# A delta-rule inverse built from 32-row blocks, w_ada sums issued beside the recurrence, and four scored blocks at the opening of the expert stage

## The chip, the cores and the metric

The kernel runs on one core of a Trainium2 chip. The metric is device time in microseconds (us) from the first to the last instruction, as the median of several runs. PE is TensorE, DVE VectorE, ACT ScalarE, POOL GpSimd, and SP the engine that issues most DMAs.

## What is computed

One decoder layer on 512 tokens of width 1024. Four parts of it matter here:

```python
mod = silu(c) @ w_ada + b_ada                      # six vectors of 1024: shifts, scales, gates
# gated delta rule, by chunks: a unit lower-triangular system for each chunk and head
a_mat = eye + where(strict, kk, 0.0)
sol = triangular_solve(a_mat, [v * beta, kb * exp(gc)])
v_new = u_c - w_c @ state                          # a recurrence over the chunks
o = q_c @ state + attn @ v_new
# PEER: 8 heads pick 16 of 128 x 128 single-neuron experts for each token
act = gelu(h @ expert_u[ids]);  ff = (gates * act) @ expert_v[ids]
x = x + gt2 * ff;  return rms_norm(x, final_norm_w)
```

The kernel uses chunks of 128 tokens (four) for the delta rule, and handles the experts densely for three token tiles (384 tokens): it scores all 128 blocks of 128 experts, multiplies the scores by a gate matrix that is zero where an expert wasn't picked, and adds up the values. The fourth token tile is gathered row by row on POOL and DVE.

## The kernel before

The stages follow one another: normalisation with the first 16 of 48 w_ada sums, projections with the short convolution, the decays and key comparison of each chunk (`decays`, `compare`), the inverse, the recurrence over the chunks, the gMLP and output projection, routing, the building of the gates (with the scores of 47 "early" blocks, written to DRAM as `sgd`), and the expert stage.

**The inverse (L436 to L477).** Each of 16 systems (4 chunks by 4 heads) is a 128x128 matrix `LS`. The inverse `X` and its transpose `Z` grow by doubling, in seven levels: at level `l` the block of `LS` that the mask `lvl[:, l]` lets through (`ms`, DVE, 128x512 for a chunk) is multiplied with `X` (`py`, L456), copied to `Y` by ACT, and multiplied with `Z` and `X` (`pz` L465, `px` L469); DVE adds the changed halves (L471, L473). All are 128x128 by 128x128 products in fp32, which the trace lists as two records each. The seven masks are made in the normalisation stage (L271 to L276). Between the chunks of each level stands a step of `later_sums`: a load of 512 KB of w_ada by SP into one of two buffers and a DVE product with a sum (L204), 32 in all.

**The recurrence (L536 to L600).** Per chunk there are products of 128x128 in fp32 with DVE and ACT steps between. `advance(fill, 13)` issues, after each chunk, 13 steps of projections that don't depend on it (`silu_z`, `gelu_v`, `token_v`); a step of a projection is three matmuls of 512 columns.

**The expert stage (L938 on).** For block `b`: `load_u`, `split_u` (ACT makes the high part, DVE the low part), `expert_scores` (24 matmuls of 384 columns into `pS`, then gelu to `sgl`; a "new" block is scored here, an early one is read back as `sgr`), `gated` (DVE product with the gates, ACT `ahi`, DVE `alo`), `split_v` (`vhi`, `vlo`), and `expert_values` (18 products of 512 columns into `acc`). `kinds` sets which blocks are early. `load_a` loads the gates for eight blocks at a time (1536 KB, DRAM `gd`). `score_ahead` scores two blocks ahead of the values. `finish` adds the residual, normalises and stores a token tile.

**What sets the order.** On PE the order is written by hand from the delta rule to the end; in the expert stage all engines are. In the delta-rule stage a scheduler orders DVE, ACT, POOL and SP.

Of the kernel before, what the change touches and what calls it, by code (L numbers as in the profile page):

```python
# [10 lines left out]
F32 = mybir.dt.float32  # L11
# [13 lines left out]
KD = D // P  # L25
EPS = 1e-6
H = 4
# [10 lines left out]
LAST = 3  # L38
SPARE = 5
# [17 lines left out]
def layer(ctx: ExitStack, tc: tile.TileContext, I, out):  # L57
# [88 lines left out]
    with ExitStack() as mixer:  # L146
# [13 lines left out]
        lvl = act.tile([P, 7, P], F32, name="lvl")  # L160
        ints = uT[:, 3].rearrange("p (a b) -> p a b", a=4).bitcast(I32)
        pi, fi, sj, si = (ints[:, i] for i in range(4))
        nc.gpsimd.iota(pi, pattern=[[0, P]], base=0, channel_multiplier=1)
        nc.gpsimd.iota(fi, pattern=[[1, P]], base=0, channel_multiplier=0)
# [44 lines left out]
        with ExitStack() as n1, tc.manual_schedule(engines={nc.vector.engine}):  # L209
# [61 lines left out]
            for l in range(7):  # L271
                nc.vector.tensor_scalar(sj, pi, l, None, op0=OP.logical_shift_right)
                nc.vector.tensor_scalar(si, fi, l, 1, op0=OP.logical_shift_right, op1=OP.bitwise_xor)
                same = zT[:, 0, :P]
                nc.vector.tensor_tensor(same, si, sj, op=OP.is_equal)
                nc.vector.scalar_tensor_tensor(lvl[:, l], same, -1.0, m2[:, 0], op0=OP.mult, op1=OP.mult)  # L276


        with ExitStack() as gdn, tc.manual_schedule(engines={nc.tensor.engine}):
# [88 lines left out]
            att, X, Z, Y, LS = ([gc_.tile(HP, F32, name=f"{nm}{n}") for n in range(NT)] for nm in ("at", "X", "Z", "Y", "ls"))  # L368
# [70 lines left out]
            idh = bc(ident[:, None, :], HP)  # L439

            def halves(x, l):
                return x.rearrange("p a (b two m) -> p a b two m", two=2, m=2 ** l)


            wad = gdn.enter_context(pool("wad2", 2))
            msum = t4("msum")[:, 0, :32]
            later_sums = mod_sums(range(16, 48), wad, msum, 16)
            for l in range(7):
                for n in range(NT):
                    if l:  # L450
                        advance(later_sums, 1 if n else 2)
                    ms = g2.tile(HP, F32, tag="ms", name="ms", bufs=4)
                    nc.vector.tensor_tensor(ms, LS[n], bc(lvl[:, l:l + 1, :], HP), op=OP.mult)
                    py = bank("py")
                    for h in range(H):
                        mm(py[:, h * P:(h + 1) * P], ms[:, h], X[n][:, h] if l else ident, start=True, stop=True)  # L456
                    if l == 0:
                        nc.vector.tensor_tensor(X[n], heads(py), idh, op=OP.add)
                        nc.vector.tensor_tensor(Z[n], ms, idh, op=OP.add)
                    else:  # L460
                        nc.scalar.copy(flat(Y[n]), py)
                for n in range(NT) if l else ():
                    pz = bank("pz")
                    for h in range(H):
                        mm(pz[:, h * P:(h + 1) * P], Y[n][:, h], Z[n][:, h], start=True, stop=True)  # L465
                    if l < 6:
                        px = bank("px")
                        for h in range(H):
                            mm(px[:, h * P:(h + 1) * P], Z[n][:, h], Y[n][:, h], start=True, stop=True)  # L469
                        xe = halves(X[n], l)[:, :, :, 0]  # L470
                        nc.vector.tensor_tensor(xe, xe, halves(heads(px), l)[:, :, :, 0], op=OP.add)  # L471
                    zo = halves(Z[n], l)[:, :, :, 1]
                    nc.vector.tensor_tensor(zo, zo, halves(heads(pz), l)[:, :, :, 1], op=OP.add)  # L473
# [715 lines left out]
```

## Time and profile before

| | us |
|---|---|
| median of 3 runs (1647.06 to 1648.66) | 1648.52 |
| the profiled execution | 1648.68 |
| its span, first to last instruction | 1647.0 |
| PE busy | 1564.7 |
| DVE busy | 1308.4 |
| ACT busy | 642.7 |

The span is the time that the profiler saw; what lies around it was 1.7 us in that execution. In the trace, an idle time is shown behind the instruction that ended it, with the instruction or transfer that was waited for. The granted clock is the TensorE clock that the throttle let through (1.00 is 2.4 GHz, 0.50 is 1.2 GHz).

### The profile page before, as it was taken

The page shows a single profiled execution, that of the slowest core. Times are in us where ns is not written, and L with a number is a line of the kernel's source. Part 1 is how long each engine was busy: PE and PEld are TensorE (multiplying, and loading weights), DVE is VectorE, ACT ScalarE, POOL GpSimd, SP SyncE. Part 2 cuts the span into 40 slices and gives each one's busy share as a digit, 9 for nine tenths or more (in the row PEclk, how much of TensorE's full clock was granted, in tenths as well). Part 3 has the DMA queues.
Part 4 walks back from the last instruction along what each step waited for, and adds up shares of the span by engine and source line. Part 5 has one row for each costly group of instructions (what it writes and reads, how often), then busy time and mean ns, then how long its engine had stood idle before and what let it go on. Part 6 is the DMA issues. An engine that isn't in the chain of part 4 may idle for free.

```text
span 1647.0 us, 22971 instructions
## 1 busy us (share of the span) xinstructions
PE 1564.7 (95%) x8567; PEld 1382.6 (84%) x8567; DVE 1308.4 (79%) x2463; ACT 642.7 (39%) x928; POOL 478.8 (29%) x355
## 2 busy tenths in 40 slices
PE   5898989999998989997999999999999999999996
PEld 3687978877897978896888888888888888888884
DVE  7989954646999999974688887888887888887756
ACT  4641224344345545562333333333333333333333
POOL 0000000005436600001244444445444444544201
PEclk9998999999998999998999999999999999999998
DMA  9223632334214567767899999999999999998753
GB/s 359 66 66 129 205 125 77 102 132 168 85 43 130 159 222 290 278 264 265 288 336 328 349 354 321 325 340 364 319 342 333 361 333 329 345 355 319 252 186 125
DMA packets 133394, 402.31 MB, mean 244 GB/s; under 512 B 12449, under 2 KB 49185, under 8 KB 131618
## 3 DMA queue, kind: packets, MB, share of 16 engines
q1 hardware_dynamic: 95106, 261.89, 44.3%
q0 software_dynamic: 38176, 138.95, 23.8%
q8 instruction: 67, 1.10, 0.3%
q14 instruction: 45, 0.37, 0.1%
HBM read 362.19 MB, written 38.60 MB: 243 GB/s over the span
## 4 chain that ended last, share of the span: by engine, by line
PE 81%; DVE 10%; DMA 5%; ACT 2%; issue 1%; POOL 1%; SPq 0%; DVEq 0%; ACTq 0%; POOLq 0%
PE pS L75 10%; PE acc L76 10%; PE acc L77 10%; PE pS L77 10%; PE acc L75 10%; PE pS L76 10%; DMA wada<-in_w_ada_c 3%; PE pp L76 3%; PE pp L75 3%; PE pp L77 3%; DVE wada L204 2%; PE pq L76 2%; PE pq L77 2%; PE pq L75 2%; PE pgb L915 1%
## 5 line engine op out<-in xcount | busy, mean ns | idle before, releaser
L972 POOL DMA_INDIRECT u_rows<-in_u_rows,rows x128 | 204.8, 1600 | 562.1 <-DVE dots L979 341.9
L75 PE MATMUL pS<-hhi,uhi 128*128 128x384 f32 x1024 | 356.6, 348 | 1.3 <-ACT uhi L731 1.3
L77 PE MATMUL pS<-hhi,ulo 128*128 128x384 f32 x1024 | 349.6, 341 | 6.1 <-POOL ulo L80 6.1
L76 PE MATMUL pS<-hlo,uhi 128*128 128x384 f32 x1024 | 348.3, 340 | 0.0
L75 PE MATMUL acc<-vhi,ahi 128*128 128x512 f32 x768 | 301.1, 392 | 14.1 <-ACT vhi L1035 14.0
L76 PE MATMUL acc<-vlo,ahi 128*128 128x512 f32 x768 | 302.5, 394 | 1.7 <-DVE vlo L80 1.7
L77 PE MATMUL acc<-vhi,alo 128*128 128x512 f32 x768 | 302.4, 394 | 0.0
L77 PEld LDWEIGHTS pS<-hhi,ulo 128*128 128x128 f32 x1024 | 193.8, 189 | 7.4 <-POOL ulo L80 7.4
L75 PEld LDWEIGHTS pS<-hhi,uhi 128*128 128x128 f32 x1024 | 194.0, 189 | 5.0 <-ACT uhi L731 2.0
L76 PEld LDWEIGHTS pS<-hlo,uhi 128*128 128x128 f32 x1024 | 194.2, 190 | 3.7
L80 DVE TENSOR_TENSOR vlo<-vraw,vhi 128x1024 fp32r<-128x1024 f32 x128 | 156.8, 1226 | 50.0 <-ACT vhi L1035 50.0
L1022 ACT CAST ahi<-a 128x384 fp32r<-128x384 f32 x128 | 65.7, 513 | 332.9 <-DVE a L1020 332.9
L75 PEld LDWEIGHTS acc<-vhi,ahi 128*128 128x128 f32 x768 | 145.4, 189 | 43.8 <-ACT vhi L1035 15.2
L76 PEld LDWEIGHTS acc<-vlo,ahi 128*128 128x128 f32 x768 | 145.1, 189 | 31.8 <-DVE vlo L80 3.0
L77 PEld LDWEIGHTS acc<-vhi,alo 128*128 128x128 f32 x768 | 145.2, 189 | 30.4
L972 POOL DMA_INDIRECT v_rows<-in_v_rows,rows x128 | 149.1, 1165 | 73.9 <-issue 35.6
L989 DVE SCALAR_TENSOR_TENSOR facc<-v_rows,dots,facc 128x1024 f32<-128x1024 f32 x128 | 164.7, 1287 | 0.6
L979 DVE CUSTOM_DVE_ANT_0 junk<-u_rows,h2tok 128x1024 bf16<-128x1024 f32 x128 | 156.0, 1219 | 0.1
L731 ACT CAST uhi<-uraw 128x1024 fp32r<-128x1024 f32 x128 | 133.6, 1047 | 39.0 <-PE pS L76 34.1
L80 POOL TENSOR_TENSOR wlo<-raw,whi 128x1024 fp32r<-128x1024 f32 x14 | 33.7, 2408 | 393.7 <-PE ptx L661 358.8
L751 ACT ACTIVATE sgl<-pS 128x384 f32<-128x384 f32 x128 | 62.6, 489 | 218.4 <-PE pS L77 214.9
L1035 ACT CAST vhi<-vraw 128x1024 fp32r<-128x1024 f32 x128 | 133.9, 1047 | 0.0
(321 smaller groups left out, 2549.8 us busy)
## 6 DMA issues: line engine op xcount, KB each, us to landing
uraw<-in_u_t SPq DMA_DIRECT2D x128, 512.0 KB, 6.4
vraw<-in_v_rows SPq DMA_DIRECT2D x125, 512.0 KB, 5.7
wada<-in_w_ada_c SPq DMA_DIRECT2D x48, 512.0 KB, 4.3
gd<-scs SPq DMA_DIRECT2D x12, 2048.0 KB, 6.6
gates<-gd SPq DMA_DIRECT2D x16, 1536.0 KB, 12.1
raw<-in_w_in_t SPq DMA_DIRECT2D x24, 512.0 KB, 3.3
sgd<-sgl SPq DMA_DIRECT2D x47, 192.0 KB, 3.9
sgr<-sgd SPq DMA_DIRECT2D x47, 192.0 KB, 5.8
```

The source lines that it names most:

```text
L75: mm(o, ahi, bhi, start=start, stop=False)
L76: mm(o, ahi, blo, start=False, stop=False)
L77: mm(o, alo, bhi, start=False, stop=stop)
L80: eng.tensor_tensor(lo, full, hi.bitcast(F32), op=OP.subtract)
L204: nc.vector.tensor_tensor_reduce(w, w, scB, scale=1.0, scalar=0.0 if bias is None else bias[:, c:c + 1], op0=OP.mult, op1=OP.add, accum_ou ...
L731: nc.scalar.copy(hi, raw)
L751: nc.scalar.activation(sgl, pS[:, :TD], AF.Gelu_apprx_tanh)
L972: nc.gpsimd.indirect_dma_start(out=r, out_offset=None, in_=I[src], in_offset=bass.IndirectOffsetOnAxis(ap=rows_[:, j:j + 1], axis=0))
L979: nc.vector.tensor_tensor_reduce(junk, rowsin.pop(("u_rows", j)), h2tok, scale=1.0, scalar=0.0, op0=OP.mult, op1=OP.add, accum_out=dots[j ...
L989: nc.vector.scalar_tensor_tensor(facc, rowsin.pop(("v_rows", j)), d[:, j % GP:j % GP + 1], facc, op0=OP.mult, op1=OP.add)
L1022: nc.scalar.copy(ahi, a)
L1035: nc.scalar.copy(hi, raw)
```

## The change

1. The inverse starts from 32x32 diagonal blocks. The first five levels multiply the masked matrix (`inner`) with right operands of only 32 columns per system (`xc`, `yc`: the four diagonal blocks of a system side by side); `Z` is written as a block-diagonal matrix by DVE's 32x32 transposes (`transposed`) and eight copies per level, half on ACT. Level 5 makes the blocks between neighbours (`py5`, `px5`, `pz5`, 32 columns), level 6 the last corner (`py6`, `pz6`, 64 columns). Zeros are written once by POOL. The masks shrink to 32 columns (`lvl`, `eye`, `blk`).
2. `fill` starts earlier: 16 steps stand within the inverse, and `advance(fill, 10)` follows each chunk instead of 13.
3. `later_sums` stands behind the inverse in the program and adds the bias itself.
4. The expert stage scores four new blocks (`LEAD`) before the first values, loads the first eight blocks' gates in two halves, and issues `score_ahead(n + 4)` behind the values of `n`. The first four blocks are all new ones.
5. At the end, values and scores of the last two blocks (`aside`) are loaded early into buffers no longer needed, and `finish` multiplies by the norm's weight on DVE only.

```diff
+B = 32
+LEAD = 4
...
-        lvl = act.tile([P, 7, P], F32, name="lvl")
+        lvl = act.tile([P, 5, B], F32, name="lvl")
+        eye = act.tile([P, B], F32, name="eye")
+        blk = act.tile([P, 3, NT], F32, name="blk")
...
-            for l in range(7):
-                nc.vector.tensor_scalar(sj, pi, l, None, op0=OP.logical_shift_right)
+            same, more = zT[:, 0, :B], zT[:, 0, B:2 * B]
+            nc.vector.tensor_scalar(pq, pi, B - 1, None, op0=OP.bitwise_and)
+            nc.vector.tensor_tensor(eye, pq, fi, op=OP.is_equal)
+            nc.vector.tensor_tensor(more, pq, fi, op=OP.is_gt)
+            for l in range(5):
+                nc.vector.tensor_scalar(sj, pq, l, None, op0=OP.logical_shift_right)
...
-                nc.vector.scalar_tensor_tensor(lvl[:, l], same, -1.0, m2[:, 0], op0=OP.mult, op1=OP.mult)
+                nc.vector.scalar_tensor_tensor(lvl[:, l], same, -1.0, more, op0=OP.mult, op1=OP.mult)
...
+            nc.vector.tensor_tensor(blk[:, 0], pb, fi[:, :NT], op=OP.is_equal)
...
+            nc.vector.tensor_tensor(more, fi[:, :NT], pb, op=OP.is_gt)
+            nc.vector.scalar_tensor_tensor(blk[:, 1], same, -1.0, more, op0=OP.mult, op1=OP.mult)
...
-            att, X, Z, Y, LS = ([gc_.tile(HP, F32, name=f"{nm}{n}") for n in range(NT)] for nm in ("at", "X", "Z", "Y", "ls"))
+            att, X, LS = ([gc_.tile(HP, F32, name=f"{nm}{n}") for n in range(NT)] for nm in ("at", "X", "ls"))
+            YY, ZZ = ([gc_.tile([P, 2, H, P], F32, name=f"{nm}{q}") for q in range(2)] for nm in "YZ")
+            Y, Z = ([x[n // 2][:, n % 2] for n in range(NT)] for x in (YY, ZZ))
...
-            msum = t4("msum")[:, 0, :32]
-            later_sums = mod_sums(range(16, 48), wad, msum, 16)
-            for l in range(7):
...
-                        advance(later_sums, 1 if n else 2)
-                    ms = g2.tile(HP, F32, tag="ms", name="ms", bufs=4)
-                    nc.vector.tensor_tensor(ms, LS[n], bc(lvl[:, l:l + 1, :], HP), op=OP.mult)
-                    py = bank("py")
...
-                        mm(py[:, h * P:(h + 1) * P], ms[:, h], X[n][:, h] if l else ident, start=True, stop=True)
...
-                        nc.vector.tensor_tensor(X[n], heads(py), idh, op=OP.add)
...
-                        nc.scalar.copy(flat(Y[n]), py)
...
-                    pz = bank("pz")
...
-                        px = bank("px")
...
-                        nc.vector.tensor_tensor(xe, xe, halves(heads(px), l)[:, :, :, 0], op=OP.add)
...
-                    nc.vector.tensor_tensor(zo, zo, halves(heads(pz), l)[:, :, :, 1], op=OP.add)
-            advance(later_sums)
-            nc.vector.tensor_tensor(mod[:, 16:48], msum, b_ada[:, 16:48], op=OP.add)
...
+            BP = [P, 2 * H, B]
+            small = lambda x: [flat(x)[:, q * 2 * H * B:(q + 1) * 2 * H * B].rearrange("p (a b) -> p a b", b=B) for q in range(2)]
+            xc, yc, tc_ = small(X[2]), small(X[3]), small(gcol("tc", HP))
+            both = lambda x: x.rearrange("p a h b -> p (a h) b")
+            blocks = lambda x: x.rearrange("p h (a b) -> p h a b", a=NT)
+            Y5, X6 = YY, [flat(X[q]).rearrange("p (a b) -> p a b", b=64) for q in range(2)]
+            for q in range(2):
+                for x in (ZZ[q], Y5[q], X6[q]):
+                    nc.gpsimd.memset(x, 0.0)
+            inner, next5 = [], []
+            for n in range(NT):
+                for dst, i, kept in ((g2.tile(HP, F32, tag="ms", name="ms", bufs=4), 0, inner), (t4("next5"), 1, next5)):
+                    nc.vector.tensor_tensor(blocks(dst), blocks(LS[n]), bc(blk[:, i][:, None, :, None], [P, H, NT, B]), op=OP.mult)
+                    kept.append(dst)
+            def products(name, q, left, right, width=B):
+                o = bank(name)
+                for j in range(2):
+                    for h in range(H):
+                        i = j * H + h
+                        mm(o[:, i * width:(i + 1) * width], left(2 * q + j, h), right(i), start=True, stop=True)
+                return o[:, :2 * H * width].rearrange("p (a b) -> p a b", b=width)
+            def transposed(q):
+                nc.vector.transpose(flat(tc_[q]), flat(xc[q]))
+                for b in range(NT):
+                    rows_b = slice(b * B, (b + 1) * B)
+                    dst = both(ZZ[q])[rows_b, :, rows_b]
+                    (nc.vector.tensor_copy if b % 2 else nc.scalar.copy)(dst, tc_[q][rows_b])
+            for l in range(5):
+                pys = [products("py", q, lambda n, h: inner[n][:, h], (lambda i: xc[q][:, i]) if l else (lambda i: eye)) for q in range(2)]
+                for q in range(2):
+                    nc.vector.tensor_tensor(yc[q], pys[q], bc(lvl[:, l:l + 1], BP), op=OP.mult)
+                advance(fill, 1)
+                if l == 0:
+                    for q in range(2):
+                        nc.vector.tensor_tensor(xc[q], yc[q], bc(eye[:, None], BP), op=OP.add)
+                else:
+                    pxs = [products("px", q, lambda n, h: Z[n][:, h], lambda i: yc[q][:, i]) for q in range(2)]
+                    for q in range(2):
+                        nc.vector.tensor_tensor(xc[q], xc[q], pxs[q], op=OP.add)
+                for q in range(2):
+                    transposed(q)
+                advance(fill, 1)
+            odd, even = (1, 3), (0, 2)
+            part = lambda b: slice(b * B, (b + 1) * B)
+            pys = [products("py5", q, lambda n, h: next5[n][:, h], lambda i: xc[q][:, i]) for q in range(2)]
+            for q in range(2):
+                for b in odd:
+                    (nc.vector.tensor_copy if b == 1 else nc.scalar.copy)(both(Y5[q])[part(b), :, part(b - 1)], pys[q][part(b)])
+                nc.vector.tensor_copy(X6[q][:B, :, :B], xc[q][:B])
+                nc.scalar.copy(X6[q][part(1), :, part(1)], xc[q][part(1)])
+            advance(fill, 2)
+            pxs = [products("px5", q, lambda n, h: Z[n][:, h], lambda i: both(Y5[q])[:, i, :B]) for q in range(2)]
+            pzs = [products("pz5", q, lambda n, h: Y5[q][:, n % 2, h], lambda i: tc_[q][:, i]) for q in range(2)]
+            for q in range(2):
+                nc.scalar.copy(X6[q][part(1), :, :B], pxs[q][part(1)])
+                for b in even:
+                    (nc.scalar.copy if b else nc.vector.tensor_copy)(both(ZZ[q])[part(b), :, part(b + 1)], pzs[q][part(b)])
+            advance(fill, 2)
+            low, high = slice(0, 64), slice(64, P)
+            pys = [products("py6", q, lambda n, h: LS[n][low, h], lambda i: X6[q][low, i], 64) for q in range(2)]
+            ys = []
+            for q in range(2):
+                ys.append(t4("y6")[high].rearrange("p a b -> p (a b)").rearrange("p (a b) -> p a b", b=64))
+                nc.scalar.mul(ys[q], pys[q][high], -1.0)
+            advance(fill, 2)
+            for q in range(2):
+                pz = bank("pz6")
+                for i in range(2 * H):
+                    mm(pz[low, i * 64:(i + 1) * 64], ys[q][:, i], both(ZZ[q])[high, i, high], start=True, stop=True)
+                nc.vector.tensor_copy(both(ZZ[q])[low, :, high], pz[low].rearrange("p (a b) -> p a b", b=64))
+            wad = gdn.enter_context(pool("wad2", 2))
+            later_sums = mod_sums(range(16, 48), wad, mod, bias=b_ada)
...
-                advance(fill, 13)
+                advance(fill, 10)
+                advance(later_sums, 5)
...
+                advance(later_sums, 3)
...
-    sp = ctx.enter_context(pool("sp", 3, side="right"))
-    kinds, pre = [], 0
-    for n in range(NK - NPRE):
+    sp = ctx.enter_context(pool("sp", LEAD, side="right"))
+    kinds, pre = [False] * LEAD, 0
+    for n in range(NK - NPRE - LEAD):
...
-        while pre < NPRE - HOLD and pre * (NK - NPRE) <= n * (NPRE - HOLD):
+        while pre < NPRE - HOLD and pre * (NK - NPRE - LEAD) <= n * (NPRE - HOLD):
...
-        def load_a(b):
+        def load_a(b, place=None):
...
-                sgl = ap_.tile([P, TD], F32, tag="sgr", name="sgr", bufs=3)
+                sgl = place or ap_.tile([P, TD], F32, tag="sgr", name="sgr", bufs=3)
...
             if b % GB == 0:
...
-                nc.sync.dma_start(groups[b // GB], gview[:, :, b:b + GB])
+                for half in range(2) if b == 0 else ():
+                    nc.sync.dma_start(groups[0][:, :, half * GB // 2:(half + 1) * GB // 2],
+                                      gview[:, :, half * GB // 2:(half + 1) * GB // 2])
+                if b:
+                    nc.sync.dma_start(groups[b // GB], gview[:, :, b:b + GB])
...
-        def load_v(b, eng=nc.sync):
-            raw = vp.tile([P, D], F32, tag="vraw", name="vraw", bufs=3)
+        def load_v(b, eng=nc.sync, place=None):
+            raw = place or vp.tile([P, D], F32, tag="vraw", name="vraw", bufs=3)
...
-            yield
-            for i, cs in enumerate(halves):
-                (nc.vector if i else nc.gpsimd).tensor_tensor(y[:, cs], x2[:, cs], fnw[:, cs], op=OP.mult)
+                nc.vector.tensor_tensor(y[:, cs], x2[:, cs], fnw[:, cs], op=OP.mult)
+                yield
...
+        load_u(new[3])
...
-        def score_ahead(b):
+        def score_ahead(b, split=True):
...
-                if nnew + 2 < len(new) and nnew:
+                if 1 < nnew < len(new) - 2:
...
-                if nnew + 1 < len(new) and nnew:
+                if 0 < nnew < len(new) - 1 and split:
...
+        for b in range(LEAD):
+            score_ahead(b, b < LEAD - 1)
+        split_v(0)
...
-            score_ahead(b)
...
-        split_v(0)
+        split_u(new[LEAD], nc.vector)
+        aside = (NK - 2, NK - 1)
...
-            score_ahead(n + 2)
-            if n + 3 < NK:
+            if n + 3 < NK and n + 3 not in aside:
...
             if n == NK - LAST - SPARE:
...
+                assert all(kinds[n + LEAD:])
+                for b in aside:
+                    load_v(b, place=up.tile([P, KD, NK], F32, tag="uraw", name="vlast").rearrange("p a b -> p (a b)"))
+                    load_a(b, sp.tile([P, TD], F32, tag="sgl", name="slast"))
...
             expert_values(n, n == 0)
+            score_ahead(n + LEAD)
```

What the change moves on an engine, from three places. On PE, at the end of the comparisons and the start of the inverse (`pa` is the last comparison, `pp` a projection). Before:

```order
L425 MATMUL pa<-qT,kT 128x128 x4
L456 MATMUL py<-ident,ms 128x128 x16
L456 MATMUL py<-X_505,ms 128x128 x4
L456 MATMUL py<-X_506,ms 128x128 x4
L456 MATMUL py<-X_507,ms 128x128 x4
L456 MATMUL py<-X_508,ms 128x128 x4
L465 MATMUL pz<-Z_509,Y_513 128x128 x4
L469 MATMUL px<-Y_513,Z_509 128x128 x4
```

Of the change:

```order
L443 MATMUL pa<-qT,kT 128x128 x4
L498 MATMUL py<-eye,ms 128x32 x16
L77 MATMUL pp<-hhi,whi 128x512
L78 MATMUL pp<-hlo,whi 128x512
L79 MATMUL pp<-hhi,wlo 128x512
L77 MATMUL pp<-hhi,whi 128x512
L78 MATMUL pp<-hlo,whi 128x512
L79 MATMUL pp<-hhi,wlo 128x512
L498 MATMUL py<-X_511,ms 128x32 x16
L77 MATMUL pp<-hhi,whi 128x512
L78 MATMUL pp<-hlo,whi 128x512
L79 MATMUL pp<-hhi,wlo 128x512
```

Products of 32 columns stand in place of those of 128, with projection steps between the groups.

On DVE, in the convolutions ahead of the inverse (`tmp` is the convolution's sum, `wlo` the low part of a weight). Before:

```order
L80 TENSOR_TENSOR wlo<-raw,whi 128x1024 x2
L192 TENSOR_SCALAR tmp<-tmp,cols 128x512
L194 SCALAR_TENSOR_TENSOR tmp<-tmp,cols 128x511
L194 SCALAR_TENSOR_TENSOR tmp<-tmp,cols 128x510
L194 SCALAR_TENSOR_TENSOR tmp<-tmp,cols 128x509
```

Of the change:

```order
L82 TENSOR_TENSOR wlo<-raw,whi 128x1024
L209 ISA wada,mod<-wada,h2tok,cols 128x1024
L209 ISA mod 128x1
L197 TENSOR_SCALAR tmp<-tmp,cols 128x512
L82 TENSOR_TENSOR wlo<-raw,whi 128x1024
L199 SCALAR_TENSOR_TENSOR tmp<-tmp,cols 128x511
L209 ISA wada,mod<-wada,h2tok,cols 128x1024
L209 ISA mod 128x1
L199 SCALAR_TENSOR_TENSOR tmp<-tmp,cols 128x510
L209 ISA wada,mod<-wada,h2tok,cols 128x1024
L209 ISA mod 128x1
L199 SCALAR_TENSOR_TENSOR tmp<-tmp,cols 128x509
```

The w_ada sums (L204 before, L209 now; two rows each) have moved up among them. In all, the order of the change has 14 of the 32 ahead of the first addition of the inverse, 7 within it and 11 behind it; before, none stood ahead of it.

On SP, at the opening of the expert stage. Before:

```order
L919 DMA gd<-scs 128x4096
L754 DMA sgd<-sgl 128x384
L1013 DMA gates<-gd 128x12x256
L1009 DMA sgr<-sgd 128x384
L725 DMA uraw<-in_u_t 128x1024
L1029 DMA vraw<-in_v_rows 128x1024
```

Of the change:

```order
L982 DMA gd<-scs 128x4096
L817 DMA sgd<-sgl 128x384
L1077 DMA gates<-gd 128x12x128 x2
L788 DMA uraw<-in_u_t 128x1024 x2
L1096 DMA vraw<-in_v_rows 128x1024
```

The gates are two transfers, the read-back of a score is gone from this place, and two loads of `u` follow at once.

## Rows read from the trace of the kernel before

**Rows 1.** Stretches: length, busy us of PE, PEld, DVE, ACT, POOL, PEclk, DMA share, GB/s.

```profile
45.00:136.00 91.00, 82.53 (x444) 68.64 (x443) 80.66 (x238) 46.37 (x66) 0.00 (x0) 0.98 0.20 64
136.00:150.00 14.00, 8.61 (x40) 8.31 (x41) 13.16 (x23) 1.76 (x3) 0.00 (x0) 0.63 0.42 134
150.00:210.00 60.00, 58.67 (x519) 58.09 (x519) 53.84 (x108) 12.33 (x21) 0.00 (x0) 1.00 0.65 215
210.00:285.00 75.00, 69.62 (x384) 58.81 (x383) 37.05 (x83) 22.95 (x32) 0.00 (x0) 0.98 0.25 85
764.00:771.00 7.00, 6.54 (x15) 4.79 (x16) 6.39 (x9) 2.84 (x5) 1.93 (x2) 0.51 0.65 235
800.00:1600.00 800.00, 800.00 (x3916) 714.77 (x3915) 645.70 (x812) 280.94 (x399) 345.14 (x249) 1.00 0.91 327
```

**Rows 2.** Groups by line, PE, 130 to 210 us: busy, mean ns | idle before.

```profile
L456 PE MATMUL py<-X,ms 128*128 128x128 f32 x192 | 25.8, 298 | 2.0 <-DVE ms L453 2.0
L465 PE MATMUL pz<-Z,Y 128*128 128x128 f32 x192 | 25.1, 276 | 1.3 <-DVE X L471 1.3
L469 PE MATMUL px<-Y,Z 128*128 128x128 f32 x160 | 21.1, 275 | 0.0
L456 PE MATMUL py<-ident,ms 128*128 128x128 f32 x32 | 4.9, 316 | 5.1 <-DVE ms L453 5.1
```

**Rows 3.** Timeline of PE: start, length [idle before]; matmuls overlap, so starts count.

```profile
76.55 0.36 PE L384 MATMUL pg<-g,m 128*128 128x16 f32 x2 [2.57 <-DVE g L341]
76.76 0.37 PE L385 MATMUL pg<-g,later 128*128 128x16 f32 x2
...
143.47 6.75 PE L456 MATMUL py<-X,ms 128*128 128x128 f32 x32 [2.02 <-DVE ms L453]
150.05 1.06 PE L465 MATMUL pz<-Z,Y 128*128 128x128 f32 x8
150.94 1.06 PE L469 MATMUL px<-Y,Z 128*128 128x128 f32 x8
...
210.14 0.40 PE L76 MATMUL pp<-hlo,whi 128*128 128x512 f32 x1
210.37 0.39 PE L77 MATMUL pp<-hhi,wlo 128*128 128x512 f32 x1
```

**Rows 4.** One line's instructions: ns least/median/most, first and last start.

```profile
L626 PE MATMUL pgm<-X,vn x64: 272/273/323, 303.2 to 306.6; 128*64 128x128 f32 x64
```

**Rows 5.** Groups by line, DVE, 135.8 to 224 us, then 45 to 136 us.

```profile
L204 DVE CUSTOM_DVE_ANT_0 wada<-wada,h2tok 128x1024 f32<-128x1024 f32 x32 | 39.2, 1224 | 8.3 <-DMA wada<-in_w_ada_c 8.2
L471 DVE TENSOR_TENSOR X<-X,px 128x256 f32<-128x256 f32 x20 | 8.3, 416 | 0.6 <-PE px L469 0.6
...
L275 DVE TENSOR_TENSOR zT<-uT 128x128 f32<-128x128 int32 x7 | 2.0, 286 | 0.1
```

**Rows 6.** Waits of PE, 128 to 290 us: total, times, longest.

```profile
PE pu L530 <- DVE vb L504: 2.2, 1, 2.2
PE pw L516 <- DVE kbe L507: 1.9, 1, 1.9
```

**Rows 7.** Timelines at the opening of the expert stage: SP, DVE, PE.

```profile
752.19 0.38 SPq L1013 DMA_DIRECT2D gates<-gd  x1
...
760.17 0.56 DVE L1020 TENSOR_TENSOR a<-sgl,gates 128x384 f32<-128x384 f32 x1 [19.67 <-DMA sgr<-sgd]
...
752.67 0.34 PE L76 MATMUL pS<-hlo,uhi 128*128 128x384 f32 x1
752.85 0.34 PE L77 MATMUL pS<-hhi,ulo 128*128 128x384 f32 x1
763.88 0.80 PE L75 MATMUL acc<-vhi,ahi 128*128 128x512 f32 x1 [10.69 <-ACT vhi L1035]
```

**Rows 8.** Waits of PE, 1595 to 1647 us.

```profile
PE acc L75 <- ACT vhi L1035: 3.3, 1, 3.3
PE acc L76 <- DVE vlo L80: 1.2, 2, 0.8
```

More of the change, by code (lines that the diff above doesn't have):

```diff
@@ L157, in layer @@
         ab = act.tile([P, NT, 8], F32, name="ab")
-        lvl = act.tile([P, 7, P], F32, name="lvl")
[L161 to L164, printed above, removed]
+        lvl = act.tile([P, 5, B], F32, name="lvl")
+        eye = act.tile([P, B], F32, name="eye")
+        blk = act.tile([P, 3, NT], F32, name="blk")
+        ints = uT[:, 3].rearrange("p (a b) -> p a b", a=16).bitcast(I32)
+        pi, fi, pq, sj, si = (ints[:, i] for i in range(5))
+        nc.gpsimd.iota(pi, pattern=[[0, B]], base=0, channel_multiplier=1)
+        nc.gpsimd.iota(fi, pattern=[[1, B]], base=0, channel_multiplier=0)
         scB = h2tok
@@ L270, in layer @@
                     wk1 = both_weights(wst, *wk1)
-            for l in range(7):
-                nc.vector.tensor_scalar(sj, pi, l, None, op0=OP.logical_shift_right)
+            same, more = zT[:, 0, :B], zT[:, 0, B:2 * B]
[4 more added lines that the diff above has]
+                nc.vector.tensor_scalar(sj, pq, l, None, op0=OP.logical_shift_right)
                 nc.vector.tensor_scalar(si, fi, l, 1, op0=OP.logical_shift_right, op1=OP.bitwise_xor)
-                same = zT[:, 0, :P]
                 nc.vector.tensor_tensor(same, si, sj, op=OP.is_equal)
-                nc.vector.scalar_tensor_tensor(lvl[:, l], same, -1.0, m2[:, 0], op0=OP.mult, op1=OP.mult)
+                nc.vector.scalar_tensor_tensor(lvl[:, l], same, -1.0, more, op0=OP.mult, op1=OP.mult)
+            same, more, pb, pn = same[:, :NT], more[:, :NT], sj[:, :NT], si[:, :NT]
+            nc.vector.tensor_scalar(pb, pi[:, :NT], 5, None, op0=OP.logical_shift_right)
+            nc.vector.tensor_scalar(pn, pi[:, :NT], 5, 1, op0=OP.logical_shift_right, op1=OP.bitwise_xor)
+            nc.vector.tensor_tensor(blk[:, 0], pb, fi[:, :NT], op=OP.is_equal)
+            nc.vector.tensor_tensor(same, pn, fi[:, :NT], op=OP.is_equal)
+            nc.vector.tensor_tensor(more, fi[:, :NT], pb, op=OP.is_gt)
+            nc.vector.scalar_tensor_tensor(blk[:, 1], same, -1.0, more, op0=OP.mult, op1=OP.mult)
+            nc.vector.tensor_tensor(blk[:, 2], same, blk[:, 1], op=OP.add)
         with ExitStack() as gdn, tc.manual_schedule(engines={nc.tensor.engine}):
```

18 lines of the change are left out of this document (removed).

## Prediction

> **What bounds the kernel now.** I read the stretches first, then what ended PE's idle time in each. From 800 to 1600 us PE is busy 800.00 of 800 us at a granted clock of 1.00 [rows 1]: nothing is to be had in the middle of the expert stage, and the change takes no matmul out of it. What can move lies at its two ends and ahead of it. In the inverse PE is again nearly full (58.67 of 60 us, 150 to 210 [rows 1]), so fewer or cheaper products shorten it. From 45 to 136 us DVE has 80.66 busy of 91 and PE 82.53 [rows 1]: two engines that are almost full, where added work has little room. At the opening of the expert stage PE waits once, for 10.69 us [rows 7]; at the end it waits 3.3 and 1.2 us [rows 8].
>
> **The inverse's products.** PE executes 192 + 192 + 160 + 32 = 576 records of 128x128 [rows 2]. Eight of them start every 0.89 us at the full clock (150.05 to 150.94), 0.112 us each [rows 3]. The change has 16 products, so 32 records, in level 0, 64 in each of levels 1 to 4, 96 in level 5 and 64 in level 6: 448. That they are narrow doesn't cheapen them by itself: two records that stream only 16 columns through 128x128 weights take from 76.55 to 76.76 us, 0.105 each [rows 3]. So the weights' load sets the pace. The last 32 records have weights of 64 columns; 64 such records start within 303.2 to 306.6 us, 0.053 each [rows 4]. Sum: 416 x 0.112 + 32 x 0.053 = 48.3 against 576 x 0.112 = 64.5, **16.2 us less**; at the dear end, without the cheaper corner, 14.3 less.
>
> The Trainium skill (TensorE: Matmul & The Clock Gate, "Wait — 56ns, not 53.3ns?") gives 25 ns from start to start for matmuls of 32 columns. By that price alone the 448 records would take 11 us and the sum would fall by another 37. The 16-column rows speak against it; the same page ("LDWEIGHTS (loading the stationary operand)") lets a load cost by its columns, which agrees with 0.105 and 0.053 us above.
>
> **Waits in the inverse.** Before, PE idles 5.1, 2.0 and 1.3 us there [rows 2], and at 139 to 150 us it runs at half clock (32 records in 6.75 us instead of 3.6 [rows 3]; clock 0.63 in 136 to 150 [rows 1]): 8.4 + 3.2 = 11.6 us. In the change the first `py` still waits for DVE's last comparison and mask, and so does the clock; the later waits are covered, since 16 fill steps (about 0.70 us each, three starts 0.23 apart [rows 3]) stand between the groups. DVE's work per level is small beside some 8.6 us of PE: four additions of 0.42 [rows 5], two transposes, four copies. No transpose and no 32-partition copy is in the trace; the nearest rows are 128x256 at 0.42 and 128x128 at 0.29 [rows 5], so six of them cost 1.7 to 2.5 us, and a level's chain stays under 5 us even doubled. I keep 8.6 of the 11.6 us: **-3** (bounds 0 and -10).
>
> **The fill.** The steps are the same; 16 move into the inverse. They leave the recurrence 10 per chunk, 7.0 us of cover instead of 9.1. PE is short of 5.4 us in 210 to 285 [rows 1], 4.1 of it in two waits for DVE [rows 6]. I take **+2** for the thinner cover (bounds -3, were both waits to go, and +6, 2.1 us lost in three chunks).
>
> **w_ada.** All 32 sums stand at 136 to 224 us before, 1.22 us each [rows 5], beside a PE that is full. In the change 14 stand ahead of the inverse's first addition: 14 x 1.22 = 17.1 us of DVE work. The masks get smaller: 28 operations of up to 0.29 us (8 us at most [rows 5]) become 30 tiny ones; I take 3 off. So 14.1 us are added where DVE has 10.3 us of idle time [rows 1], of which a sum can use only pieces. The inverse starts late by at least 14.1 - 10.3 = 3.8 us and at most 14.1, plus what a `raw` weight load loses behind a w_ada load on SP's queue that waits for one of two buffers. I take the middle: **+7** (bounds 3.8 and 15). The 18 sums taken out of the inverse give nothing back: PE was the bound beside them.
>
> **Opening of the expert stage.** PE scores until 753.2 and starts the values at 763.88; the gates' load is issued at 752.19 and the first gated product runs at 760.17, after which the split of `v` follows [rows 7]. Then 15 matmuls run at clock 0.51 in 764 to 771 [rows 1], 0.43 us each instead of 0.23: 3 us. That is 13.7 us. In the change two more blocks are scored first, 48 matmuls at the 0.18 us between 752.67 and 752.85 [rows 7], 8.6 us, so PE is busy to 761.8; `v` is split earlier; and half of the gates (768 KB) suffices. At half of the 8 us from issue to product it lands about 757, and `ahi`, `alo` follow within 2 us. The two scored blocks aren't extra work: their scores move from the steady stretch, which is PE-bound. I keep 0.7 us of waiting: **-13** (bounds -5, if the two loads of `u` push the gates to 766, and -13.7).
>
> **The end.** Waits of 3.3 + 1.2 us [rows 8] and a second spell at half clock of about the same price as at the opening, 2.7: 7.2 us. With the last two blocks loaded early most of this goes; the multiplication in `finish` moves from POOL to DVE, 0.7 us beside a PE that still works, except in the last tile, where I put 0. **-5.5** (bounds 0 and -7.2).
>
> **Sum.** -16.2 - 3 + 2 + 7 - 13 - 5.5 = -28.7 us. Against the profiled execution, 1648.68, which is the median (1648.52) to within 0.2: **1620 us**. With every term at its good end (-16.2 - 10 - 3 + 3.8 - 13.7 - 7.2 = -46) it would be 1602, at its bad end (-14.3 + 0 + 6 + 15 - 5 + 0 = +2) 1650.
>
> **Rivals.** *The inverse at half clock.* At half clock a 128x128 record takes 0.21 (6.75 us / 32 [rows 3]) and a fill step 1.3. The inverse would take 448 x 0.21 + 16 x 1.3 = 115 us instead of 48.3 + 11.2 + 3.2 = 63: +52, so 1672 us, **slower**. It decides once more than 28.7/52 = 55% of the inverse runs so. For it: the clock was low in 136 to 150 although PE was busy 8.61 of 14 us [rows 1], and no row shows narrow products for longer than a microsecond, so that nothing here says whether they hold or raise the clock. Against it: the inverse of before ran at 1.00 through 60 us of products whose pace was also set by the weights [rows 1], and full-width fill stands in every gap. The Trainium skill (TensorE: Matmul & The Clock Gate, "Part 4: PE-mode transpose") says of one kind of matmul that it doesn't count as busy time for the clock in the same way; whether narrow products are treated so no run here shows.
>
> *DVE ahead of the inverse.* All 14 sums in full, the weight loads late behind them, and thin cover later: +15 and +6 in place of +7 and +2 give 1632 us, still faster.
>
> *The opening gains little.* Two more loads of `u` (1 MB) ahead of the gates, at the 327 GB/s of the steady stretch [rows 1], delay them by 3.2 us; if PE waits and the clock falls again, -5 in place of -13: 1628 us.
>
> **How the numbers follow.** Forecast with its own spread 0.50, DVE rival 0.12, opening rival 0.07, half clock 0.26, and 0.05 that losses of several kinds cancel the gain. The half-clock case has a share below its break-even, which I leave where it is. Within 0.2% (3.3 us, about what a measurement of this kernel can tell from no change): 0.05. Faster 0.69, slower 0.26. The likeliest case's own range is 1606 to 1634. The range for 8 in 10 has to take in most of the half-clock case: 1606 to 1674.
>
> **What would show it.** Right: about 50 us between the first `py` and `pv` less the fill, at clock 1.00; the first `py` some 7 us later than 132.7 to 139 us; the first `acc` within 1 us of the last score at the opening and no fall of the clock there; no wait over 1 us before 1636 less the gain. Wrong: records of 32 columns 0.21 apart, or far below 0.1; projections of 60 to 130 us waiting for `raw`; a `gates` wait of several us; DMA share of 1 with PE gaps after 770 us, since the same bytes must come in less time.

## The result, and the profile after

The change is slower. Its median is 1664.99 us (1662.07 to 1665.57, 4 runs) against 1647.79 us for the kernel before on the same chips: ratio 1.0092, 95% interval 1.0078 to 1.0106 (the quotient of the two medians is 1.0104; both say slower). I had forecast 1620 us. The profiled execution, which the rows below come from, took 1662.07 us with a span of 1660.4; the other three took about 3 us more.

The loss stands in one place. On the page of the change, the line of the granted clock in 40 slices (41.5 us each) has a dip in slices 4 to 6:

```profile
PEclk9997569999999999999999999999999999999998
```

Stretches of the change in the columns of [rows 1] (length, busy us of PE, PEld, DVE, ACT, POOL, granted clock, DMA share, GB/s):

```profile
140.00:150.00 10.00, 6.76 (x35) 6.18 (x36) 8.63 (x21) 1.77 (x5) 0.00 (x0) 0.66 0.00 0
150.00:160.00 10.00, 10.00 (x50) 9.61 (x50) 2.54 (x7) 0.00 (x0) 0.00 (x0) 0.56 0.31 107
160.00:210.00 50.00, 50.00 (x217) 48.07 (x215) 15.39 (x40) 7.86 (x18) 0.00 (x0) 0.50 0.08 24
230.00:240.00 10.00, 10.00 (x39) 8.83 (x39) 2.34 (x4) 1.43 (x3) 0.00 (x0) 0.50 0.15 41
250.00:260.00 10.00, 10.00 (x59) 8.65 (x59) 8.64 (x21) 3.31 (x5) 0.00 (x0) 1.00 0.60 207
```

From 160 to 210 us PE is busy all the time, DVE about a third of it, ACT a sixth: PE waits for nobody, and yet the clock is at 0.50, its lower level of 1.2 GHz. Before, the same stage ran at 1.00 (150 to 210 in [rows 1]).

The timeline of PE in the change (start, length, idle before), projections left out, to be held against [rows 3]:

```profile
136.50 2.76 PE L498 MATMUL py<-eye,ms 128*128 128x32 f32 x24
143.24 1.91 PE L498 MATMUL py<-eye,ms 128*128 128x32 f32 x8 [3.98 <-DVE ms L489]
147.67 3.75 PE L498 MATMUL py<-X,ms 128*128 128x32 f32 x32
152.67 6.87 PE L498 MATMUL px<-X,Z 128*128 128x32 f32 x32
160.77 6.87 PE L498 MATMUL py<-X,ms 128*128 128x32 f32 x32
168.88 6.87 PE L498 MATMUL px<-X,Z 128*128 128x32 f32 x32
...
241.92 2.72 PE L551 MATMUL pz<-Z,y 64*64 64x64 f32 x32
244.57 0.66 PE L563 MATMUL pv<-ident,vT 128*128 128x128 f32 x4
```

Behind the wait of 3.98 us the clock was low until about 147.6. The group at 147.67 takes 3.75 us for 32 records, the pace of the full clock; the next and all that follow in levels 1 to 4 take 6.87. So the clock came up once among the narrow products and went down again while PE was working without a gap.

A ledger by marks that both traces have, in us of the span:

| mark | before | change | difference |
|---|---|---|---|
| py after the wait for DVE's last mask | 139.37 | 143.24 | +3.9 |
| first pv, the end of the inverse | 209.46 | 244.57 | +35.1 |
| pss of the second norm | 358.7 | 377.2 | +18.5 |
| last gate product (pgb) | 743.4 | 762.0 | +18.6 |
| last acc | 1636.3 | 1650.2 | +13.9 |

The marks are of the profiled execution, whose span is 13.4 us longer than before; the medians differ by 17.2. So the inverse lost 31 us, the recurrence and the gMLP gave back 17 (11 of them are the 16 projection steps that moved into the inverse), and the expert stage gained less than 5, not 18.5. The wait at its opening is shorter and has another releaser than in [rows 7]; the waits at the end ([rows 8]) are as long as before. Waits of PE in the change, 740 to 790 and 1590 to 1665 us:

```profile
PE acc L77 <- ACT ahi L1089: 3.8, 1, 3.8
...
PE acc L77 <- ACT vhi L1102: 2.5, 2, 1.2
PE acc L78 <- DVE vlo L82: 1.8, 3, 0.8
```

### The profile page after: what moved, and what is told of

Read it like the earlier page. It is cut to its first block, busy times and chain, and to the rows that moved or that the text cites. A ratio compares the mean times of both kernels' runs of the same rounds, so it can differ in the third digit from the quotient of the medians.

```text
span 1660.4 us, 22700 instructions
## 1 busy us (share of the span) xinstructions
PE 1588.9 (96%) x8439; PEld 1403.0 (84%) x8439; DVE 1298.6 (78%) x2454; ACT 636.9 (38%) x935; POOL 480.2 (29%) x357
## 4 chain that ended last, share of the span: by engine, by line
PE 81%; DVE 10%; issue 3%; ACT 3%; DMA 2%; POOL 0%; SPq 0%; ACTq 0%; DVEq 0%; POOLq 0%
PE pS L77 10%; PE pS L79 10%; PE pS L78 10%; PE acc L78 9%; PE acc L79 9%; PE acc L77 9%; PE pp L77 3%; PE pp L78 3%; PE pp L79 3%; PE py L498 2%; PE px L498 2%; PE pq L78 2%; PE pq L79 2%; PE pq L77 2%; PE pgb L978 1%
## 5 line engine op out<-in xcount | busy, mean ns | idle before, releaser
L82 DVE TENSOR_TENSOR ulo<-uraw,uhi 128x1024 fp32r<-128x1024 f32 x105 | 128.4, 1223 | 49.4 <-ACT uhi L794 49.4
L82 DVE TENSOR_TENSOR alo<-a,ahi 128x384 fp32r<-128x384 f32 x128 | 71.5, 559 | 74.2 <-ACT ahi L1089 74.2
## 6 DMA issues: line engine op xcount, KB each, us to landing
gates<-gd SPq DMA_DIRECT2D x15, 1536.0 KB, 13.4
```

The lines of the kernel that those rows point to most:

```text
L82: eng.tensor_tensor(lo, full, hi.bitcast(F32), op=OP.subtract)
```

## The experiments

| kernel | median us | ratio to before, 95% interval |
|---|---|---|
| the change | 1664.99 | 1.0092 (1.0078 to 1.0106) |
| inverse_only | 1666.95 | 1.0130 (1.0089 to 1.0170) |
| expert_only | 1641.21 | 0.9969 (0.9957 to 0.9981) |
| wide128 | 1623.88 | 0.9864 (0.9845 to 0.9883) |
| wide64 | 1623.69 | one run |
| fill3 | 1657.14 | one run |
| narrow_cover | 1661.80 | one run |
| no_sums | 1618.93 | one run |
| open_fix | 1617.13 | 0.9813 (0.9793 to 0.9832) |
| both_fix | 1616.39 | 0.9812 (0.9793 to 0.9832) |
| best | 1617.02 | 0.9811 (0.9785 to 0.9837) |

The kernels were timed on different chips, on which the median of the kernel before was 1646.5 to 1647.8 us: medians of two rows are comparable to about 1 us at best.

The theory was that the narrow products themselves bring the clock down. Its rivals were the wait ahead of the inverse, the zeros in the operands, and a price per record that has nothing to do with the clock.

### Wide128 and wide64: the same products, streamed wider

```diff
-                        mm(o[:, i * width:(i + 1) * width], left(2 * q + j, h), right(i), start=True, stop=True)
+                        times = min(128, 512 - i * width) // width
+                        x = right(i)
+                        mm(o[:, i * width:(i + times) * width].rearrange("p (a b) -> p a b", b=width), left(2 * q + j, h),
+                           bc(x[:, None, :], [x.shape[0], times, width]), start=True, stop=True)
```

Wide64 has 64 in place of 128.

> The change, but each product of the inverse's levels 0 to 6 (py, px, pz of 32 columns) streams its right operand four times over, 128 columns in all (py6: twice); the extra columns are written over by the next product. Same records, weights, order and zeros, same result. Theory A (PE's clock stays at half in the inverse because the products stream so few columns): the granted clock is 1.00 from 150 us to the end of the inverse, records 0.112 us apart, the inverse takes about 63 us instead of 101, total about 1627 us. Theory B (the half clock comes from something else of this order: the wait ahead of the inverse, the zeros in the operands, the waits between groups): still 0.50 there and 1665 us. Theory C (each record costs its weights and its columns, so wider is dearer): over 1665 us.

> As wide128 but each 32-column operand is streamed twice, 64 columns. Theory A: somewhere between, with stretches at either level of the clock, or all of one of them: 1627 to 1665 us. Theory B and C: 0.50 throughout and 1665 us or more.

Wide128 took 1623.88 us, wide64 1623.69. The timeline of PE in wide128, and its stretches:

```profile
144.32 2.08 PE L500 MATMUL py<-eye,ms 128*128 128x128 f32 x8 [3.90 <-DVE ms L489]
148.75 4.10 PE L500 MATMUL py<-X,ms 128*128 128x128 f32 x32
153.41 3.73 PE L500 MATMUL px<-X,Z 128*128 128x128 f32 x32
157.67 3.73 PE L500 MATMUL py<-X,ms 128*128 128x128 f32 x32
...
205.62 0.65 PE L566 MATMUL pv<-ident,vT 128*128 128x128 f32 x4
```

```profile
140.00:150.00 10.00, 6.10 (x26) 5.33 (x26) 9.89 (x23) 2.24 (x5) 0.00 (x0) 0.66 0.16 52
150.00:160.00 10.00, 10.00 (x85) 9.73 (x84) 8.10 (x19) 1.61 (x4) 0.00 (x0) 1.00 0.62 209
160.00:200.00 40.00, 39.08 (x314) 36.98 (x313) 30.70 (x66) 9.37 (x22) 0.00 (x0) 1.00 0.56 185
```

And wide64:

```profile
160.00:200.00 40.00, 40.00 (x326) 38.38 (x326) 24.67 (x56) 9.96 (x23) 0.00 (x0) 1.00 0.39 130
```

The same number of products with the same weights, order and zeros, and the same wait of 3.9 us ahead of them, runs at 1.00, and the inverse takes 61.3 us (144.32 to 205.62) instead of 101.3. Streaming four times the columns costs nothing at the full clock: 32 records take 3.73 us here and 3.75 in the full-speed group of level 1 of the change. That the zeros or the price of a record were the cause is excluded. One other thing moved: the scheduler put 18 of the w_ada sums beside the inverse in wide128, 7 in the change. No_sums, below, has none there and runs at 1.00 too, so they aren't the cause. I had expected 1627 us; the median came 41 us below that of the change, not 38.

One group of wide64 does not fit the columns alone. The first group of level 6 has 64 columns in the change and in wide64 (128 in most of its products in wide128), and its weights have 64 rows instead of 128. In wide64, its row of the timeline and a stretch behind it:

```profile
197.18 3.92 PE L500 MATMUL py<-X,ls 64*128 64x64 f32 x32
202.00:204.00 2.00, 2.00 (x6) 1.10 (x5) 0.09 (x2) 0.43 (x1) 0.00 (x0) 0.50 0.62 164
```

Behind it the clock of wide64 falls to 0.50 for about 3 us, with PE busy; in wide128 it stays at 1.00 there. So 64 columns went with the full clock where the weights had 128 rows, and with a fall where they had 64; why, no run shows.

### Narrow_cover: no wait ahead of the inverse

```diff
+            advance(fill, 6)
             for l in range(5):
...
-                advance(fill, 10)
+                advance(fill, 9)
```

> The change with its narrow products, and six projection steps ahead of the inverse's first product. Theory A (the narrow products themselves bring the clock down): it enters the inverse at 1.00 and falls within the first levels, and the inverse runs at half clock as in the change: 1658 to 1665 us. Theory B (the 4 us wait ahead of the inverse brings the clock down and the inverse only fails to raise it): without the wait it stays at 1.00, 1620 to 1630 us.

It took 1661.80 us. Its stretches, and PE's timeline there:

```profile
140.00:145.00 5.00, 5.00 (x39) 4.59 (x37) 5.00 (x13) 0.63 (x1) 0.00 (x0) 1.00 0.00 0
145.00:150.00 5.00, 5.00 (x41) 4.73 (x40) 3.71 (x12) 3.00 (x6) 0.00 (x0) 1.00 0.00 0
150.00:155.00 5.00, 5.00 (x26) 4.71 (x25) 1.56 (x2) 0.15 (x1) 0.00 (x0) 0.56 0.33 108
155.00:160.00 5.00, 5.00 (x22) 4.71 (x22) 1.79 (x5) 0.51 (x2) 0.00 (x0) 0.50 0.00 0
```

```profile
146.92 3.65 PE L498 MATMUL py<-X,ms 128*128 128x32 f32 x32
151.70 6.87 PE L498 MATMUL px<-X,Z 128*128 128x32 f32 x32
```

PE doesn't wait once from 130 to 250 us (busy 120.00 of 120), enters the inverse at 1.00, and the clock falls all the same, between 150 and 151 us, behind the second narrow group. The wait ahead of the inverse isn't the cause.

The Trainium skill (TensorE: Matmul & The Clock Gate, "HAM oscillation — how this bites in real kernels") gives as the rule against a low clock that PE should have no long idle gaps. By that rule this kernel would have kept the full clock; it had no gap and lost it, so the rule isn't enough here. What the Trainium skill (same page, "Part 4: PE-mode transpose") says about transposes, that they don't count as busy in the same way, has a counterpart in these rows for ordinary products of 32 columns.

### Fill3: three projection steps between the narrow groups instead of one

```diff
-                advance(fill, 1)
+                advance(fill, 3)
...
-                advance(fill, 10)
+                advance(fill, 5)
```

> The change with its narrow products, but three projection steps (nine matmuls of 512 columns) between their groups in levels 0 to 4 instead of one, and 5 instead of 10 per chunk in the recurrence. Theory A (what PE streams between the narrow products decides the clock): the clock rises in the inverse and stays up for most or all of it, 1625 to 1640 us. Theory B (the narrow products hold the clock down whatever stands between them): half clock through the inverse, 1665 us or more, as the added fill runs at half clock too.

1657.14 us, between the two theories. Its stretches:

```profile
160.00:168.00 8.00, 8.00 (x64) 7.60 (x64) 5.10 (x12) 1.61 (x4) 0.00 (x0) 1.00 0.25 80
168.00:172.00 4.00, 4.00 (x15) 3.19 (x14) 1.62 (x3) 0.00 (x0) 0.00 (x0) 0.57 0.48 177
172.00:175.00 3.00, 3.00 (x29) 3.00 (x28) 0.86 (x2) 0.07 (x1) 0.00 (x0) 1.00 0.18 74
175.00:179.00 4.00, 4.00 (x15) 3.28 (x15) 3.09 (x8) 2.48 (x5) 0.00 (x0) 0.57 0.02 4
183.00:209.00 26.00, 26.00 (x97) 23.39 (x96) 9.90 (x19) 3.25 (x6) 0.00 (x0) 0.50 0.25 81
210.00:220.00 10.00, 10.00 (x66) 9.17 (x66) 3.43 (x11) 2.78 (x7) 0.00 (x0) 0.82 0.23 79
```

The clock falls first at about 168 us, 17 us later than in the change (151), swings between its two levels until 183, stays low until 209 and swings on. Wide work between the narrow groups delays the fall but doesn't prevent it here, and while the clock is down the added projections run at half speed too. Neither theory's number came true. What stands between the narrow groups makes a difference; how the clock weighs it stays open.

### Inverse_only and expert_only: the two halves apart

The edits are the halves of the diff: everything ahead of the expert stage, or the expert stage alone.

> Only the part of the change ahead of the expert stage (inverse, fill, w_ada, masks); the expert stage as before. Theory A: the stage up to the routing ends 18.6 us later than before, as in the change, and nothing after it differs: about 1666 us. If the expert stage of the change loses time of its own, this is faster than the change by more than a few us.

> Only the expert stage's part of the change; the inverse and w_ada as before. From the two traces: the opening gains 7 us of waiting and 3 us of half clock less one new spell at half clock, the end gains little: 1641 to 1645 us. By the prediction's terms (-13 and -5.5) it would be 1630 us.

1666.95 and 1641.21 us: the halves add up to the change (+20 and -6 against +17), within what such medians can tell (inverse_only's four runs spread from 1663.84 to 1676.35). In expert_only PE waits as in the change (740 to 820, 800 to 1595 and 1590 to 1675 us):

```profile
PE acc L76 <- ACT ahi L1027: 3.8, 1, 3.8
...
PE pS L78 <- DVE ulo L81: 1.5, 4, 0.5
...
PE acc L76 <- ACT vhi L1040: 2.5, 2, 1.2
PE acc L77 <- DVE vlo L81: 1.8, 3, 0.8
```

So the gain of 18.5 us that I had put on the expert stage was 5.5. At the opening 14.1 us (10.69 and 0.46 of waits, 2.9 of half clock) became 6.7 (3.8 and 2.9): 7.3. At the end the prediction's 7.2 us became 7.0 (4.3 of waits and again some 2.7 at half clock): 0.2. And 1.5 us of waits for `ulo` are new in the steady stretch, where before had none.

### Open_fix: what was waited for at the opening

On DVE in the change, the product `a` that the first values wait for stands behind `vlo`, and that behind ACT's `vhi`:

```profile
773.38 1.23 DVE L82 TENSOR_TENSOR ulo<-uraw,uhi 128x1024 fp32r<-128x1024 f32 x1 [3.02 <-ACT uhi L794]
781.86 1.23 DVE L82 TENSOR_TENSOR vlo<-vraw,vhi 128x1024 fp32r<-128x1024 f32 x1 [7.25 <-ACT vhi L1102]
783.00 0.55 DVE L1087 TENSOR_TENSOR a<-sgl,gates 128x384 f32<-128x384 f32 x1
```

ACT's `vhi` stands behind the gelu of the fourth block's scores, which PE ends at 780. The edit, on top of wide128:

```diff
-        for b in range(LEAD):
-            score_ahead(b, b < LEAD - 1)
-        split_v(0)
-        for b in range(2):
-            gated(b)
+        for b in range(LEAD - 1):
+            score_ahead(b)
+        split_v(0)
+        gated(0)
+        score_ahead(LEAD - 1, False)
+        gated(1)
```

> Wide128, with the split of v and the gated product of block 0 issued ahead of the fourth block's scores instead of behind them. Theory A (the opening's remaining wait of 3.8 us is an order on ACT: vhi, and with it a and ahi, stands behind the gelu of the fourth block's scores): the wait goes and with it the spell at half clock behind it, 3.8 + 2.9 = 6.7 us less than wide128, about 1617 us. Theory B (the gates' transfer is what comes last): the first values start no earlier, 1624 us.

1617.13 us, 6.75 less than wide128, as expected. ACT now makes `vhi` right behind the third block's gelu, and `vlo` follows it (first row); `a` follows without a wait for the gates, and PE has no gap from 700 to 760 us:

```profile
740.16 1.22 DVE L82 TENSOR_TENSOR vlo<-vraw,vhi 128x1024 fp32r<-128x1024 f32 x1 [3.01 <-ACT vhi L1105]
741.30 0.55 DVE L1090 TENSOR_TENSOR a<-sgl,gates 128x384 f32<-128x384 f32 x1
```

```profile
700.00:760.00 60.00, 60.00 (x406) 55.09 (x405) 34.09 (x39) 27.35 (x42) 7.06 (x6) 1.00 0.79 283
```

### Both_fix and best: the end

```diff
             gated(n + 2)
+            if n == NK - LAST - 1:
+                split_v(n + 2)
+                gated(n + 3)
             expert_values(n, n == 0)
...
-        for n in range(NK - LAST, NK - 1):
-            before(n)
-            if n + 2 < NK:
-                gated(n + 2)
+        split_v(NK - 1)
```

> Open_fix, and at the end the split of v of the last block but one and the gated product of the last block are issued ahead of the last full block's values. Theory A (at the end the loads are no longer waited for, but the chain DVE a, ACT ahi, DVE alo, ACT vhi, DVE vlo of two blocks in series, 3.2 us each): most of the 4.3 us of waits at the end goes, and the spell at half clock if what is left is short: 3 to 6 us less than open_fix, 1611 to 1614 us. Theory B (the loads are late): no gain, 1617 us.

1616.39 us, no gain that can be told from none, and nearly the same waits (2.5 and 1.5 us): theory A fell. B's time came true, but not its reason: from 1560 us on neither PE, DVE nor ACT waits for a load. DVE comes to these splits late anyway; my next theory was that this is because in program order it first finishes the gathered token tile. Best moves that behind the last block's splits, and takes over the six projection steps of narrow_cover (9 instead of 10 behind each chunk):

```diff
-            if n >= NK - LAST - SPARE:
+            if n == NK - LAST - SPARE:
                 advance(picked_tile, 1)
...
         advance(picks)
-        advance(picked_tile)
...
         split_v(NK - 1)
+        advance(picked_tile)
```

> Both_fix with two moves of work that exists already: six projection steps (4.2 us) stand on PE ahead of the inverse's first product (and 9 instead of 10 behind each chunk), and DVE finishes the gathered token tile behind the last block's splits instead of ahead of them. Theory A: the 3.9 us wait ahead of the inverse is filled, the clock stays up there, and DVE reaches the last blocks' splits some 4 us earlier, so that the waits of 4 us at the end and the half clock behind them go: 4 to 7 us from the first and 3 to 6 us from the second, 1604 to 1610 us. Theory B: DVE's comparison ends later than PE's fill in any case and the finish of the gathered tile comes back as a wait of the last tiles: 1613 to 1617 us.

1617.02 us: no gain either, but the trace shows where both moves went. Starts of the values (least, median, most ns; first and last start), both_fix and then best:

```profile
L77 PE MATMUL acc<-vhi,ahi x768: 387/389/792, 740.4 to 1603.1; 128*128 128x512 f32 x192
```

```profile
L77 PE MATMUL acc<-vhi,ahi x768: 387/389/505, 739.2 to 1597.5; 128*128 128x512 f32 x192
```

PE ends 5.6 us earlier: 1.2 from the filled wait ahead of the inverse (3.9 us, but waits have come up behind it, the longest 1.6 us in the recurrence, which has fewer projection steps), the rest from shorter waits at the end (0.5 and 0.8 are left, as the theory had it, and no matmul reaches the half-clock length of 792 ns any more). But the span ends 1.6 us later, 18.2 us behind the last value instead of 11.0: DVE works from 1587 to 1592 on the gathered tile, turns to the first of the others at 1593.77, 1.9 us later than in both_fix, and has caught up with both_fix at the last (1604.64 against 1604.55). There a gap of its own follows, which is the 1.6 us:

```profile
1606.95 0.69 DVE L1133 TENSOR_TENSOR x<-y,x 128x512 f32<-128x512 f32 x1 [1.63 <-issue]
```

The chain that ended last reaches this gap through the store of an earlier tile and a load of `x` (2.26 and 2.77 us); that they cause it wasn't tried. What PE gained, the finish of the tiles behind it took back.

### No_sums: what the w_ada sums cost

```diff
-            later_sums = mod_sums(range(16, 48), wad, mod, bias=b_ada)
+            later_sums = iter(())
+            nc.vector.tensor_copy(mod[:, 16:48], b_ada[:, 16:48])
```

> Wide128 without the 32 later w_ada sums (their loads, products and sums are left out, so the later shifts, scales and gates are the bias alone). It bounds what they cost. Theory A (the 14 sums ahead of the inverse delay it by DVE work): the first wait of py ends 4 to 8 us earlier and the total falls by as much, to 1616 to 1620 us. Theory B (they fit in DVE's gaps, and the 4 us later start is of another cause): 1622 to 1625 us.

1618.93 us in its one run, 5 less than wide128. The first wait of `py` ends 3.6 us earlier than in wide128:

```profile
140.74 1.74 PE L500 MATMUL py<-eye,ms 128*128 128x128 f32 x8 [3.94 <-DVE ms L489]
```

The wait itself is as long as ever (3.94 against 3.90): PE reaches the inverse's first `py` 3.6 us earlier as well (133.96 against 137.58), so what the sums cost was spread over the stage ahead and was not in this wait. And with no w_ada sum beside the inverse the clock is as in wide128:

```profile
160.00:200.00 40.00, 40.00 (x335) 37.86 (x334) 15.04 (x37) 12.19 (x26) 0.00 (x0) 1.00 0.13 41
```

## Why the prediction was wrong

**The step that failed is the inverse at full clock: the terms -16.2 and -3, and with them the choice between the forecast and its first rival.** I put 0.50 on the full clock and 0.26 on half clock, because the inverse of before had kept 1.00 with products whose pace was also set by the weights' load, and because full-width projections stand in every gap. The first argument compared the pace of the records, which is indeed the same, 0.112 us at the full clock; but the clock didn't go by it: with products of 32 columns it fell (the change, narrow_cover), with the same products streamed over 64 or 128 it stood at 1.00 through levels 1 to 5 (wide64, wide128), and PE was busy in all four. The second didn't hold in the change or in fill3: one or three projection steps between the groups didn't keep it up. The inverse took 101.3 us where the forecast had 63, and the sign that I had named for being wrong, records of 32 columns 0.21 apart, is what the rows show (6.87 us for 32).

That the rival's 1672 us lies near the 1665 measured is partly luck. Its inverse was too dear, 115 us against 101.3: one group of level 1 ran at the full clock and one of level 5 nearly (3.75 and 3.98 us), the last group's narrower weights took 2.72, and 24 of the first records stand ahead of the mark. The fill came out better than it had it, too; the smaller gain of the expert stage made up for most of both.

**The inverse's products and waits** were right where the clock was up. In wide128 the inverse takes 61.3 us with 11.2 us of projections in it, against 70.1: -20.0 where I had -16.2 - 3. (The steps that had no row before, DVE's transposes and copies, take 0.42 and 0.29 us in the change, as the nearest rows had it; the copies on ACT take 0.40.)

**The fill** was wrong in sign: +2, measured -5.4. From the first `pv` to the `pss` of the second norm before takes 149.2 us, wide128 and the change 132.6; 11.2 of the 16.6 are the moved steps. Of the other 5.4, 3.2 are idle time of PE (6.96 us before, 3.79 in wide128): the waits of [rows 6] are gone. And before, a spell at half clock stood behind them, which the bound of -3 put at nothing:

```profile
221.00:225.00 4.00, 4.00 (x16) 3.43 (x16) 2.54 (x13) 0.59 (x1) 0.00 (x0) 0.57 0.01 2
```

At 0.57 of the full clock these 4 us lose about 1.7 (an estimate). Why the waits went wasn't tried alone: before, four w_ada sums stand on DVE between the first `pv` and `kbe`, which the second wait is for, in the change one and in wide128 none.

**w_ada:** +7, measured +5 in the one run of no_sums, and of that 3.6 at the start of the inverse. Inside its bounds.

**The opening:** -13, measured -7.3. The first half of the gates isn't what is waited for in the change: its `a` runs at 783.00 behind `vlo`. The profile puts the wait of before's first product down to `sgr`, the read-back of a score issued right behind the gates ([rows 7]), though that product reads the gates; the change drops this read-back too, and which of the two helped wasn't tried apart. The failed step is "`v` is split earlier": it stands earlier in the program than `gated`, but on ACT behind the gelu of the scores that were put ahead of it, so the split couldn't begin before PE ended them. Open_fix, which changes just that, takes 6.75 us off.

**The end:** -5.5, measured -0.2. The loads were hidden as the change means them to be (in the change no wait of PE there is ended by a load, and DVE waits 0.8 us for one), but DVE's and ACT's chain for the last blocks came last in their place. The bound of 0 covers the size, but it named no such chain. Best shows the next one in line: the finish of the tiles.

With the clock up the kernel takes 1624 us (wide128), near the forecast of 1620, but for partly other reasons. By its marks it has +5.0 at the start of the inverse, -20.0 in it, -5.4 in the fill and -5.0 in the rest, mainly the expert stage, where the sum had +7, -19.2, +2 and -18.5: the fill made good about half of what the expert stage missed.

The result beats the kernel before by nearly 2% when the change keeps its order and only streams its operands wider and splits `v` one block earlier (open_fix, 1617.13 us).

## What to carry to other kernels

Cutting the columns of a product doesn't shorten it where the weights' load sets its pace, and it can cost the clock: hold the granted clock of each stretch beside its busy time, since a PE that is busy throughout can still be at half speed. Here streaming the narrow operand several times, into columns that the next product overwrites, was free and kept the clock up (with one exception in wide64, behind the group whose weights have 64 rows). When work is moved ahead to hide a wait, follow each small step that the waiting instruction needs through its own engine's order: the gelu in front of `vhi` cost 6.75 us, about half of the 14.1 us that were to be removed.

## What was not expected of the hardware

That the clock falls with PE busy 10.00 of 10 us and no wait for over a hundred microseconds: 0.50 in the change from 160 to 210 us, where twice the columns per product (wide64) gave 1.00 from 160 to 200 with 40.00 of 40 us busy. And that a product streaming 128 columns through 128x128 weights in fp32 takes no longer than one of 32 (3.73 and 3.75 us for 32 records).
